# P times V as two 64-column tiles and softmax denominators as four 32-column tiles in a hybrid decoder trunk

## The chip, the cores and the metric

The kernel runs on all 8 cores of one Trainium2 chip (two dies, cores 0 to 3 and 4 to 7). Each core works through one of the 8 batch rows; no core waits for another. The metric is device microseconds of the slowest core, and the kernel before takes about 8,530 us.

A run can fall into a slow state: the cores of one die, or of both, show a lower granted TensorE clock and take longer. In group 1 of the experiments the kernel before took 8,528.1 us in its fast run, with all cores at a mean clock of 0.978 or 0.979, and 9,839.3 us in its slowest, with one die at 0.805 or 0.806 and the other at 0.977 to 0.979. Most runs of my experiments fell into it. I therefore give two numbers for each: its fast run, where there is one, and the median of its undisturbed cores. By undisturbed I mean the cores of a die on which all four had a mean granted clock of 0.970 or more, whatever the other die did. The kernel before shows that these can be compared: undisturbed cores took 8,453 to 8,533 us beside a slow die, and 8,457 to 8,530 us in fast runs.

The engines: PE is TensorE, ACT ScalarE, DVE VectorE, POOL GpSimd, SP SyncE (it issues most DMAs, 5,756 of 5,988 on core 4 of the kernel before). PEld in the profile is PE's loading of weights, which overlaps with matmuls: on the page of the kernel before, PE is busy for 94% of the span and PEld for 41%.

## The reference, cut to what matters

Four layers, each with an input projection, causal multi-head latent attention with 8 heads beside a short convolution, an output projection, a squared-ReLU MLP, and a gated per-layer embedding. The change touches only the attention:

```python
# SEQ = 4096, N_HEADS = 8, QK_HEAD = 96, V_HEAD = 64
sc = jnp.einsum('bqhd,bkhd->bhqk', qb, k, preferred_element_type=jnp.float32) * scale
sc = jnp.where(k_idx[None, :] <= q_idx[:, None], sc, -jnp.inf)
pr = jax.nn.softmax(sc, axis=-1).astype(v.dtype)
return jnp.einsum('bhqk,bkhd->bqhd', pr, v)
```

## The kernel before

Everything is held transposed: tokens lie along the free dimension, 512 queries to a block. For a pair of heads and a chunk of 128 keys the kernel makes scores S (keys x queries) on TensorE, takes the exponential on ScalarE into a tile `pt` (128 x 512, bf16), and multiplies V by it, accumulating over the chunks in PSUM. The denominator comes with the same matmul: V of a head pair is stored as 192 columns, `values of head 0 | 64 ones | values of head 1`, and a head uses 128 neighbouring columns. So one matmul with 128 columns of weights fills 64 rows of PSUM with values and 64 rows with the sum of the exponentials.

```python
# th_S: scores of one head and one key chunk
mm(ps, ps.ap[:, 0:n], kt.ap[0:96, hh, (kc % 4) * 128:(kc % 4) * 128 + 128],
   qt.ap[0:96, hh, qoff:TB], qr + [kt, qt], True, True, n=n)
# ... expt(): pt = exp(SCALE * ps) on ACT, triangle mask on POOL for the diagonal chunks

# th_PV: 128 columns of V and ones
mm(O[hh], O[hh].ap[:, qoff:TB], vt.ap[:, kc % 4, 64 * hh:64 * hh + 128], pt.ap[:, 0:n],
   [pt, vt], kc == 0, kc == nkc - 1, n=n)

# tail: after the last chunk of a head pair
act(rd, rd.ap[64:128], O[0].ap[64:128, :], AF.Ln, [O[0]])
act(rd, rd.ap[0:64], O[1].ap[0:64, :], AF.Ln, [O[1]])
act(re, re.ap[0:64], rd.ap[64:128], AF.Exp, [rd], scale=-1.0)
act(re, re.ap[64:128], rd.ap[0:64], AF.Exp, [rd], scale=-1.0)
tt("dve", lo, lo.ap, O[0].ap[0:64, :], re.ap[0:64], ALU.mult, [O[0], re, au])
tt("dve", hi, hi.ap, O[1].ap[64:128, :], re.ap[64:128], ALU.mult, [O[1], re, au])
# ...
```

Attention does not run alone. The program is put in order ahead of time by a list scheduler in the kernel's own Python code: projections of later blocks (A), attention (B) and output projection plus MLP of earlier blocks (C) are threads, and the scheduler gives TensorE whichever of their matmuls can start first by its table of costs. The order is then fixed for each engine. Two PSUM banks hold scores, two the accumulators of a head pair, four the rest.

Of the kernel before, what the change touches and what calls it, by code (L numbers as in the profile page):

```python
# [7 lines left out]
BF16 = mybir.dt.bfloat16  # L8
# [7 lines left out]
TB = 512  # L16
# [13 lines left out]
    return int(_GOFF[kind] + l * _GW[kind] + i)  # L30

C_ONES, C_BLK2, C_BLK16, C_KST, C_TRI = 0, 128, 256, 384, 448
NCB = 576
C_INVF, C_SGN = 576, 577
NCM = 578

def mk(method, *args, **kw):
    return lambda e: getattr(e, method)(*args, **kw)  # L38
# [357 lines left out]
def build(nl=NL, S=SEQ):  # L396
# [19 lines left out]
    QN = dram("QN", [4, 128, S])  # L416
    QR = dram("QR", [2, 128, S])
    KD = dram("KD", [2, 4, 96, NB, 2, TB])
    VD = dram("VD", [2, 4, 128, NK * 192])
    MIX = dram("MIX", [8, 128, S])  # L420
    CSD = dram("CSD", [2, NB, 8, 16, TB], F32)

    with contextlib.ExitStack() as st:
# [31 lines left out]
        okp = A.pool("ok", 3, BF16, [TB])  # L455
        ropq = A.pool("rope", 2, BF16, [TB])
        cosp = A.pool("cosp", 1, F32, [2, TB])
        vtp = A.pool("vt", 2, BF16, [4, 3, 64])
        kp = A.pool("k", 3, BF16, [2, TB], parts=96)
        vp = A.pool("v", 3, BF16, [4, 192])  # L460
        qp = A.pool("q", 2, BF16, [2, TB], parts=96)
        ptp = A.pool("pt", 6, BF16, [TB])
        aup = A.pool("au", 4, F32, [TB])
        anp = A.pool("an", 2, BF16, [TB])
        mxp = A.pool("mix", 8, BF16, [TB])
# [9 lines left out]
        tokC = Pool("tokC", [T() for _ in range(3)])  # L475
        build.sbuf = A.off

        qsub, ausub = {}, {}
        for t in qp.tiles:
            qsub[t] = (T(t.ap[0:64]), T(t.ap[64:80]), T(t.ap[80:96]))  # L480
        for t in aup.tiles:
            ausub[t] = (T(t.ap[0:64]), T(t.ap[64:128]))

        dks = {}

        def dk(*key):
# [12 lines left out]
            c = gcol(kind, l, i)  # L499
            return gp.ap[lo:hi, c:c + 1]  # L500

        def mm(ps, out, lhsT, rhs, reads, start, stop, n=TB):
            X.cur.grp.done += n / 512.0
            return P.c("pe", mk("matmul", out, lhsT=lhsT, rhs=rhs, start=start, stop=stop),
                       reads=reads, writes=[ps], n=n)
# [101 lines left out]
        P.dma("sp", mk("dma_start", out=gp.ap, in_=gpack), writes=[gp], nbytes=1 << 17)  # L607
        cms = [xp.tiles[i] for i in range(8, 10)]
        P.dma("sp", mk("dma_start", out=cms[0].ap, in_=cmat[:, 0:512]), writes=[cms[0]], nbytes=1 << 18)
        P.dma("sp", mk("dma_start", out=cms[1].ap[:, 0:64], in_=cmat[:, 512:576]), writes=[cms[1]], nbytes=1 << 15)  # L610
        P.dma("sp", mk("dma_start", out=cf.ap, in_=cmat[:, 576:578]), writes=[cf], nbytes=1 << 12)
        cb2 = T(cb.ap)
        P.c("dve", mk("tensor_copy", out=cb.ap[:, 0:512], in_=cms[0].ap), reads=[cms[0]], writes=[cb])
        P.c("dve", mk("tensor_copy", out=cb.ap[:, 512:576], in_=cms[1].ap[:, 0:64]), reads=[cms[1]], writes=[cb])
        P.c("dve", mk("memset", epsc.ap, EPS), writes=[epsc], n=1)
        for vt in vtp.tiles:
            P.c("pool", mk("memset", vt.ap, 1.0), writes=[vt], n=768)
        INVF = cf.ap[:, 0:1]
        SGN = cf.ap[0:32, 1:2]

# [100 lines left out]
        def th_A(s, grp):  # L721
# [190 lines left out]
            def vproj():  # L912
                for i in range(4):
                    ps = yield from bank(tokA, kvn, [("ukv", s)])
                    pc = bk[("ukv", s)]
                    for kc in range(2):
                        mm(ps, ps.ap[:, :], kvn[kc].ap[:, i * 128:(i + 1) * 128],
                           pc.ap[:, kc * 1024 + 512:kc * 1024 + 1024], [pc, kvn[kc]], kc == 0, kc == 1)
                    piece_use("ukv")
                    (vt,) = yield R("act", reads=[ps], acq=[vtp])  # L920
                    act(vt, vt.ap[:, :, 0:3:2, :], ps.ap[:, :].rearrange("p (a b x) -> p a b x", b=2, x=64), AF.Copy, [ps])
                    drop(ps)
                    kc_ = 4 * t + i
                    yield R("sp", reads=[vt], writes=[dk("VD", par, t)])
                    dma(VD[par][:, :, kc_ * 192:(kc_ + 1) * 192].rearrange("a p n -> p a n"),
                        vt.ap.rearrange("p a b x -> p a (b x)"), [vt], [dk("VD", par, t, i)], 1 << 18)
                    release(vtp, vt)
                    bump("V")

# [148 lines left out]
        def th_Bload():  # L1078
            for s in range(NS):
                l, t = divmod(s, NB)  # L1080
                par = l % 2
                for p in range(4):
                    (qt,) = yield R("sp", acq=[qp], evs=[("Q", s)])
                    a, b, c = qsub[qt]
                    dma(a.ap, QN[p].rearrange("(hh i) s -> i hh s", hh=2)[:, :, cols(t)], [dk("QN", t, p)], [a, qt], 1 << 17)
                    for j, tl in ((0, b), (1, c)):
                        dma(tl.ap, QR[j].rearrange("(h i) s -> i h s", i=16)[:, 2 * p:2 * p + 2, cols(t)],
                            [dk("QR", t, j)], [tl], 1 << 15)
                    bk[("q", s, p)] = qt
                    fire(("q", s, p))  # L1090
                    for cj in range(t + 1):
                        evs = [("K", s), ("V", s)] if cj == t else []
                        (kt,) = yield R("sp", acq=[kp], evs=evs)
                        kk_ = [dk("KD", par, cj, p, i) for i in range(3)]
                        dma(kt.ap, KD[par, p, :, cj], kk_, [kt], 96 * 2 * TB * 2)
                        bk[("k", s, p, cj)] = kt
                        fire(("k", s, p, cj))
                        (vt,) = yield R("sp", acq=[vp], evs=evs)
                        dma(vt.ap.rearrange("p a n -> p (a n)"), VD[par][p][:, cj * 768:(cj + 1) * 768],
                            [dk("VD", par, cj, i) for i in range(4)], [vt], 128 * 768 * 2)  # L1100
                        bk[("v", s, p, cj)] = vt
                        fire(("v", s, p, cj))

# [36 lines left out]
        def th_PV(s, grp):  # L1140
# [3 lines left out]
            aus = [None] * 4  # L1144
            q = SqSum(4)

            def tail(p, O):
                (rd,) = yield R("act", reads=O, acq=[rp])
                act(rd, rd.ap[64:128], O[0].ap[64:128, :], AF.Ln, [O[0]])
                act(rd, rd.ap[0:64], O[1].ap[0:64, :], AF.Ln, [O[1]])  # L1150
                (re,) = yield R("act", reads=[rd], acq=[rp])
                act(re, re.ap[0:64], rd.ap[64:128], AF.Exp, [rd], scale=-1.0)
                act(re, re.ap[64:128], rd.ap[0:64], AF.Exp, [rd], scale=-1.0)
                release(rp, rd)
                (au,) = yield R("dve", reads=[re] + O, acq=[aup])
                lo, hi = ausub[au]
                tt("dve", lo, lo.ap, O[0].ap[0:64, :], re.ap[0:64], ALU.mult, [O[0], re, au])
                tt("dve", hi, hi.ap, O[1].ap[64:128, :], re.ap[64:128], ALU.mult, [O[1], re, au])
                release(psO, O[0])
                release(psO, O[1])  # L1160
                release(rp, re)
                aus[p] = au
                yield from sq_add(q, au.ap, [au, lo, hi])

            def norm():
                rt = yield from rstd(q, 1.0 / 512, tokA)
                for c in range(4):
                    au = aus[c]
                    lo, hi = ausub[au]
                    (an,) = yield R("dve", reads=[lo, hi, rt], acq=[anp])  # L1170
                    stt(an, an.ap, au.ap, G(G_OA, l, c), rt.ap, ALU.mult, ALU.mult, [au, lo, hi, rt, gp])
                    lo.r.append(an.w)
                    hi.r.append(an.w)
                    release(aup, au)
                    yield R("sp", reads=[an], writes=[dk("MIX", t, c)])
                    dma(MIX[c][:, cols(t)], an.ap, [an], [dk("MIX", t, c)], 1 << 17)
                    release(anp, an)
                release(rp, rt)
                fire(("attn", s))

            spawn(norm(), grp, "bnorm")
            for p in range(4):
                O = [None, None]
                for kc in range(nkc):
                    cj = kc // 4
                    r = kc - 4 * t
                    qoff = 128 * r if r > 0 else 0
                    n = TB - qoff
                    for hh in range(2):
                        if kc == 0:  # L1190
                            (O[hh],) = yield R("pe", acq=[psO], evs=[("pt", s, i), ("v", s, p, cj)])
                        yield R("pe", evs=[("pt", s, i), ("v", s, p, cj)])
                        pt = bk.pop(("pt", s, i))
                        vt = bk[("v", s, p, cj)]
                        yield R("pe", reads=[pt, vt])
                        mm(O[hh], O[hh].ap[:, qoff:TB], vt.ap[:, kc % 4, 64 * hh:64 * hh + 128], pt.ap[:, 0:n],
                           [pt, vt], kc == 0, kc == nkc - 1, n=n)
                        release(ptp, pt)
                        i += 1
                    if kc % 4 == 3:  # L1200
                        release(vp, bk.pop(("v", s, p, cj)))
                spawn(tail(p, O), grp, "tail")
            fire(("B", s))

        def th_Bseq():
# [368 lines left out]
```

## Time and profile before

| | before |
|---|---|
| median of runs | 8,533.7 us (8,506.4 to 8,577.0, 4 runs) |
| TensorE busy | 7,994.5 us, 94% |
| ScalarE, VectorE busy | 62%, 47% |
| TensorE idle | 525.9 us |
| start to start of neighbouring 128x512 matmuls, median | 216 ns |

The page of the kernel before, its first part (busy time of each engine), the engines' line of its fourth (the chain that ended last), and TensorE's two groups of its fifth (busy us, mean ns of one, idle time before them and what ended most of it):

```profile
PE 7994.5 (94%) x36480; PEld 3514.0 (41%) x36480; DVE 3975.2 (47%) x5969; ACT 5325.5 (62%) x10023; POOL 1075.5 (13%) x1582
...
PE 77%; ACT 8%; DMA 5%; issue 4%; SPq 2%; DVE 2%; POOL 1%; ACTq 0%; DVEq 0%; POOLq 0%
...
L38 PE MATMUL ps<-arena 128*128 128x512 bf16 (+2 forms) x36480 | 7994.5, 378 | 525.9 <-ACT arena L38 220.5
L38 PEld LDWEIGHTS ps<-arena 128*128 128x128 bf16 (+2 forms) x36480 | 3514.0, 98 | 5005.9 <-issue 1147.3
```

TensorE is what the kernel waits for. The mean of 378 ns is how long the profile shows one matmul and not what it costs: the next one starts 216 ns after it, so that matmuls overlap, and the cost is these 216 ns. The stretches of 2,000 us show that this holds through the run. Columns are the stretch, its length, busy time and count of PE, PEld, DVE, ACT and POOL, then granted clock, DMA share and GB/s:

```profile
0.00:2000.00 2000.00, 1684.32 (x7388) 715.77 (x7389) 904.27 (x1385) 1254.20 (x2375) 247.98 (x411) 0.93 0.79 195
2000.00:4000.00 2000.00, 1932.44 (x8890) 853.23 (x8888) 961.67 (x1440) 1316.22 (x2492) 272.11 (x394) 0.99 0.71 196
4000.00:6000.00 2000.00, 1931.23 (x8915) 856.06 (x8914) 978.06 (x1463) 1305.71 (x2461) 271.63 (x394) 0.99 0.72 198
```

The kernel before has one place where the shape of the weights changes: the rotary key's, with eight matmuls of 64 columns and, elsewhere and alone, one of 32 rows and 64 columns. The timeline of PEld around one of these (start us, length, what, count, and the idle time before it):

```profile
3662.92 0.10 PEld L38 LDWEIGHTS ps<-arena 128*128 128x128 bf16 x1
3663.44 1.43 PEld L38 LDWEIGHTS ps<-arena 128*64 128x64 bf16 x8 [0.43 <-issue]
3665.29 0.77 PEld L38 LDWEIGHTS ps<-arena 128*128 128x128 bf16 x5 [0.41 <-issue]
```

The weight loader stands idle for over 0.4 us at the way in and at the way out. In this trace it does not load ahead across the change of shape. In the starts of the matmuls this is 309 ns from the last 128-column one to the first 64-column one, and 312 ns back, in place of 216. The lone 32-row matmul costs 309 ns in and 331 ns out.

Last, what TensorE waited for (the view of waits, core 4: total us, times, longest us):

```profile
PE ps L38 <- ACT arena L38: 220.5, 245, 15.5
PE ps L38 <- DVE arena L38: 139.4, 109, 22.4
PE ps L38 <- DMA arena<-WZ_B: 64.7, 9, 26.7
```

### The profile page before, as it was taken

What the parts mean: (1) busy time and instruction counts of PE and PEld (TensorE: products, weight loads), DVE (VectorE), ACT (ScalarE), POOL (GpSimd) and SP (SyncE); (2) the same over time, 40 slices, a digit from 0 to 9 for tenths busy, and PEclk for the clock granted to TensorE, in tenths of its full rate; (3) what the DMA queues carried; (4) which work ended last, traced back from release to release, by engine and by line L of the source; (5) the groups of instructions that cost most, each with busy time, mean ns of one, the idle gap of its engine ahead of it and who ended that gap; (6) DMA issues with size and microseconds to landing.
All of it is one profiled execution on the core that took longest, in us unless ns stands there. A gap on an engine that the chain in (4) does not pass through costs nothing.

```text
span 8529.4 us, 132287 instructions; the slowest of 8 cores (8475.2 to 8529.4 us)
## 1 busy us (share of the span) xinstructions
PE 7994.5 (94%) x36480; PEld 3514.0 (41%) x36480; DVE 3975.2 (47%) x5969; ACT 5325.5 (62%) x10023; POOL 1075.5 (13%) x1582
## 2 busy tenths in 40 slices
PE   4589999999999999999999999999999999999998
PEld 1233344444444444444444444444444444444443
DVE  3445544445554444444555544444555544443334
ACT  3457766677555677666566666767655666766523
POOL 0111111012111111101111110111111011101001
PEclk7799999999999999999999999999999999999999
DMA  9998886666888866656788875566666666655554
GB/s 179 184 206 220 222 209 179 177 185 190 216 209 212 208 195 189 184 163 180 208 224 218 214 205 171 179 187 187 183 196 179 191 184 186 182 164 169 160 171 140
DMA packets 833341, 1621.95 MB, mean 190 GB/s; under 512 B 161472, under 2 KB 436544, under 8 KB 830016
## 3 DMA queue, kind: packets, MB, share of 16 engines
q1 hardware_dynamic: 813504, 1496.31, 60.2%
q0 software_dynamic: 19136, 117.19, 9.3%
q8 instruction: 331, 5.42, 0.3%
q14 instruction: 370, 3.03, 0.1%
HBM read 1524.77 MB, written 314.31 MB: 216 GB/s over the span
## 4 chain that ended last, share of the span: by engine, by line
PE 77%; ACT 8%; DMA 5%; issue 4%; SPq 2%; DVE 2%; POOL 1%; ACTq 0%; DVEq 0%; POOLq 0%
PE ps L38 77%; ACT arena L38 8%; SPq L38 2%; DVE arena L38 2%; DMA arena<-xT 2%; DMA MIX<-arena 1%; DMA arena<-WZ_B 1%; POOL arena L38 1%; DMA QN<-arena 0%; DMA HD<-arena 0%; DMA arena<-WC_B 0%; DMA QR<-arena 0%; ACTq L200 0%; DMA VD<-arena 0%; DMA arena<-VD 0%
## 5 line engine op out<-in xcount | busy, mean ns | idle before, releaser
L38 PE MATMUL ps<-arena 128*128 128x512 bf16 (+2 forms) x36480 | 7994.5, 378 | 525.9 <-ACT arena L38 220.5
L38 PEld LDWEIGHTS ps<-arena 128*128 128x128 bf16 (+2 forms) x36480 | 3514.0, 98 | 5005.9 <-issue 1147.3
L38 ACT ACTIVATE arena<-ps 128x512 bf16<-128x512 f32 (+5 forms) x6976 | 3605.3, 573 | 2632.6 <-PE ps L38 2502.0
L38 DVE TENSOR_TENSOR arena<-arena 128x512 bf16<-128x512 f32 (+3 forms) x2176 | 1564.6, 728 | 1735.4 <-ACT arena L38 1688.1
L38 ACT ACTIVATE arena<-arena 128x512 f32<-128x512 f32 (+2 forms) x2498 | 1540.4, 629 | 462.0 <-DVE arena L38 284.5
L38 POOL TENSOR_TENSOR arena<-arena 128x128 bf16<-128x128 bf16 (+2 forms) x1344 | 944.7, 715 | 5607.6 <-ACT arena L38 3752.6
L38 DVE TENSOR_TENSOR arena<-arena,ps 128x512 f32<-128x512 f32 x1280 | 872.1, 685 | 1521.3 <-PE ps L38 1384.4
L38 DVE SCALAR_TENSOR_TENSOR arena<-arena 128x512 bf16<-128x512 f32 (+2 forms) x1540 | 1120.3, 765 | 536.4 <-ACT arena L38 324.8
L38 DVE SCALAR_TENSOR_TENSOR arena<-ps,arena 128x512 bf16<-128x512 f32 (+1 forms) x320 | 239.3, 748 | 486.8 <-ACT arena L38 444.7
L38 ACT ACTIVATE arena<-ps,arena 128x512 f32<-128x512 f32 (+1 forms) x544 | 375.2, 690 | 84.0 <-PE ps L38 82.7
L38 DVE TENSOR_TENSOR arena<-ps,arena 64x512 f32<-64x512 f32 x256 | 176.2, 688 | 249.1 <-ACT arena L38 245.0
L38 POOL DMA_DIRECT2D WC_B<-wc x164 | 85.2, 520 | 1555.8 <-PE ps L38 1467.2
L38 DVE TENSOR_SCALAR arena<-arena 128x512 f32<-128x512 f32 x135 | 65.4, 485 | 0.9 <-issue 0.2
L38 DVE COPY arena<-arena 128x2 f32<-128x2 f32 x240 | 46.5, 194 | 12.2 <-DVE arena L38 1.4
L38 POOL DMA_DIRECT2D WZ_B<-wz x24 | 13.3, 555 | 160.6 <-PE ps L38 160.6
L38 POOL DMA_DIRECT2D arena<-pT x32 | 24.6, 769 | 24.2 <-PE ps L38 18.1
L38 POOL DMA_DIRECT2D WU_B<-wu x12 | 6.7, 555 | 100.8 <-PE ps L38 82.0
L38 ACT ACT_TABLE_LOAD x5 | 6.4, 1283 | 19.0 <-DMA arena<-xT 13.8
L38 DVE CAST arena<-arena 128x512 f32<-128x512 int32 (+2 forms) x5 | 1.9, 379 | 6.8 <-DMA arena<-cmat 6.4
L38 POOL MEMSET arena<- 128x768 bf16 x2 | 1.4, 737 | 0.3 <-POOLq L400 0.3
L38 DVE MEMSET arena<- 128x2 f32 (+1 forms) x17 | 1.0, 60 | 0.0
L400 POOL MEMSET const-float32-0.0<- 128x1 f32 x1 | 0.1, 99 | 0.5 <-issue 0.5
(3 smaller groups left out, 0.3 us busy)
## 6 DMA issues: line engine op xcount, KB each, us to landing
arena<-WC_B SPq DMA_DIRECT2D x1312, 512.0 KB, 4.4
arena<-WZ_B SPq DMA_DIRECT2D x544, 256.0 KB, 4.5
arena<-KD SPq DMA_DIRECT2D x576, 192.0 KB, 4.2
arena<-VD SPq DMA_DIRECT2D x576, 192.0 KB, 4.3
WC_B<-wc POOLq DMA_DIRECT2D x164, 512.0 KB, 8.6
outT<-arena SPq DMA_DIRECT2D x256, 256.0 KB, 4.0
arena<-outT SPq DMA_DIRECT2D x192, 256.0 KB, 5.5
arena<-xT SPq DMA_DIRECT2D x160, 256.0 KB, 7.7
```

The costliest lines, as they stand in the source:

```text
L38: return lambda e: getattr(e, method)(*args, **kw)
L400: nc = bass.Bass("TRN2", target_bir_lowering=False, dynamic_dma_scratch_size=2048)
```

## The change

The intent is to stop spending 64 columns of the array on copies of one sum. The values of the two heads become two matmuls with 64 columns each, placed in different halves of the array's columns so that they might run at once. The denominators of two heads and two key chunks become four matmuls with 32 columns of ones, also side by side. If they do run at once, a head pair needs 3 slots of TensorE for two chunks in place of 4. The price: V loses its ones (128 columns, a third less to load), the denominators of even and odd chunks lie in different groups of 32 rows and must be swapped and added in the tail, and a head pair asks for both accumulator banks before its first matmul, where the kernel before asked for the second one a matmul later (both kernels hold a bank until the tail has read it).

```diff
-        vp = A.pool("v", 3, BF16, [4, 192])
+        vp = A.pool("v", 3, BF16, [4, 128])
-        ptp = A.pool("pt", 6, BF16, [TB])
+        ptp = A.pool("pt", 8, BF16, [TB])
@@ mm: the scheduler's cost of a tile is its share of a slot
-        def mm(ps, out, lhsT, rhs, reads, start, stop, n=TB):
+        def mm(ps, out, lhsT, rhs, reads, start, stop, n=TB, par=1):
+            n = n // par
@@ tail
-                (rd,) = yield R("act", reads=O, acq=[rp])
-                act(rd, rd.ap[64:128], O[0].ap[64:128, :], AF.Ln, [O[0]])
-                act(rd, rd.ap[0:64], O[1].ap[0:64, :], AF.Ln, [O[1]])
-                ...
+                (rd,) = yield R("act", reads=[Dn], acq=[rp])
+                for j in range(4):
+                    k = j ^ 1
+                    act(rd, rd.ap[32 * j:32 * j + 32], Dn.ap[32 * k:32 * k + 32, :], AF.Copy, [Dn])
+                yield R("dve", reads=[rd, Dn])
+                tt("dve", rd, rd.ap, rd.ap, Dn.ap[:, :], ALU.add, [rd, Dn])
+                release(psO, Dn)
+                yield R("act", reads=[rd])
+                act(rd, rd.ap, rd.ap, AF.Ln, [rd])
+                act(rd, rd.ap, rd.ap, AF.Exp, [rd], scale=-1.0)
+                (au,) = yield R("dve", reads=[rd, O], acq=[aup])
+                tt("dve", au, au.ap, O.ap[:, :], rd.ap, ALU.mult, [O, rd])
+                release(psO, O)
@@ th_PV
+                    if kc == 0:
+                        O, Dn = yield R("pe", acq=[psO, psO], evs=evs)
+                    yield R("pe", evs=evs)
+                    pt = [bk.pop(("pt", s, i + hh)) for hh in range(2)]
+                    ...
                     for hh in range(2):
-                        mm(O[hh], O[hh].ap[:, qoff:TB], vt.ap[:, kc % 4, 64 * hh:64 * hh + 128], pt.ap[:, 0:n], ...)
+                        mm(O, O.ap[64 * hh:64 * hh + 64, qoff:TB], vt.ap[:, kc % 4, 64 * hh:64 * hh + 64], pt[hh].ap[:, 0:n],
+                           [pt[hh], vt], kc == 0, kc == nkc - 1, n=n, par=2)
+                    pts += [(pt[hh], qoff, n) for hh in range(2)]
+                    ... # t == 0: two matmuls with zero weights open the odd quadrants
+                    if kc % 2 == 1:
+                        for j, (ptj, qo, nj) in enumerate(pts):
+                            row = 64 * (j % 2) + 32 * (j // 2)
+                            mm(Dn, Dn.ap[row:row + 32, qo:TB], ONE32, ptj.ap[:, 0:nj], [ptj, cb], kc == 1 and (t > 0 or j < 2),
+                               kc == nkc - 1, n=nj, par=4)
+                            release(ptp, ptj)
+                        pts = []
```

More of the change, by code (lines that the diff above doesn't have):

```diff
@@ L32 @@
 C_ONES, C_BLK2, C_BLK16, C_KST, C_TRI = 0, 128, 256, 384, 448
-NCB = 576
-C_INVF, C_SGN = 576, 577
-NCM = 578
+C_ZERO = 576
+NCB = 608
+C_INVF, C_SGN = 608, 609
+NCM = 610
 def mk(method, *args, **kw):
@@ L418, in build @@
     KD = dram("KD", [2, 4, 96, NB, 2, TB])
-    VD = dram("VD", [2, 4, 128, NK * 192])
+    VD = dram("VD", [2, 4, 128, NK * 128])
     MIX = dram("MIX", [8, 128, S])
@@ L457, in build @@
         cosp = A.pool("cosp", 1, F32, [2, TB])
-        vtp = A.pool("vt", 2, BF16, [4, 3, 64])
+        vtp = A.pool("vt", 2, BF16, [TB])
         kp = A.pool("k", 3, BF16, [2, TB], parts=96)
-        vp = A.pool("v", 3, BF16, [4, 192])
+        vp = A.pool("v", 3, BF16, [4, 128])
         qp = A.pool("q", 2, BF16, [2, TB], parts=96)
-        ptp = A.pool("pt", 6, BF16, [TB])
+        ptp = A.pool("pt", 8, BF16, [TB])
         aup = A.pool("au", 4, F32, [TB])
@@ L476, in build @@
         build.sbuf = A.off
-        qsub, ausub = {}, {}
+        qsub = {}
         for t in qp.tiles:
             qsub[t] = (T(t.ap[0:64]), T(t.ap[64:80]), T(t.ap[80:96]))
-        for t in aup.tiles:
-            ausub[t] = (T(t.ap[0:64]), T(t.ap[64:128]))
         dks = {}
@@ L609, in build @@
         P.dma("sp", mk("dma_start", out=cms[0].ap, in_=cmat[:, 0:512]), writes=[cms[0]], nbytes=1 << 18)
-        P.dma("sp", mk("dma_start", out=cms[1].ap[:, 0:64], in_=cmat[:, 512:576]), writes=[cms[1]], nbytes=1 << 15)
-        P.dma("sp", mk("dma_start", out=cf.ap, in_=cmat[:, 576:578]), writes=[cf], nbytes=1 << 12)
+        P.dma("sp", mk("dma_start", out=cms[1].ap[:, 0:96], in_=cmat[:, 512:608]), writes=[cms[1]], nbytes=1 << 15)
+        P.dma("sp", mk("dma_start", out=cf.ap, in_=cmat[:, 608:610]), writes=[cf], nbytes=1 << 12)
         cb2 = T(cb.ap)
         P.c("dve", mk("tensor_copy", out=cb.ap[:, 0:512], in_=cms[0].ap), reads=[cms[0]], writes=[cb])
-        P.c("dve", mk("tensor_copy", out=cb.ap[:, 512:576], in_=cms[1].ap[:, 0:64]), reads=[cms[1]], writes=[cb])
+        P.c("dve", mk("tensor_copy", out=cb.ap[:, 512:608], in_=cms[1].ap[:, 0:96]), reads=[cms[1]], writes=[cb])
         P.c("dve", mk("memset", epsc.ap, EPS), writes=[epsc], n=1)
-        for vt in vtp.tiles:
-            P.c("pool", mk("memset", vt.ap, 1.0), writes=[vt], n=768)
         INVF = cf.ap[:, 0:1]
@@ L920, in vproj @@
                     (vt,) = yield R("act", reads=[ps], acq=[vtp])
-                    act(vt, vt.ap[:, :, 0:3:2, :], ps.ap[:, :].rearrange("p (a b x) -> p a b x", b=2, x=64), AF.Copy, [ps])
+                    act(vt, vt.ap, ps.ap[:, :], AF.Copy, [ps])
                     drop(ps)
@@ L924, in vproj @@
                     yield R("sp", reads=[vt], writes=[dk("VD", par, t)])
-                    dma(VD[par][:, :, kc_ * 192:(kc_ + 1) * 192].rearrange("a p n -> p a n"),
-                        vt.ap.rearrange("p a b x -> p a (b x)"), [vt], [dk("VD", par, t, i)], 1 << 18)
+                    dma(VD[par][:, :, kc_ * 128:(kc_ + 1) * 128].rearrange("a p n -> p a n"),
+                        vt.ap.rearrange("p (a n) -> p a n", n=128), [vt], [dk("VD", par, t, i)], 1 << 17)
                     release(vtp, vt)
@@ L1098, in th_Bload @@
                         (vt,) = yield R("sp", acq=[vp], evs=evs)
-                        dma(vt.ap.rearrange("p a n -> p (a n)"), VD[par][p][:, cj * 768:(cj + 1) * 768],
-                            [dk("VD", par, cj, i) for i in range(4)], [vt], 128 * 768 * 2)
+                        dma(vt.ap.rearrange("p a n -> p (a n)"), VD[par][p][:, cj * 512:(cj + 1) * 512],
+                            [dk("VD", par, cj, i) for i in range(4)], [vt], 1 << 17)
                         bk[("v", s, p, cj)] = vt
@@ L1145, in th_PV, with tail @@
             q = SqSum(4)
-            def tail(p, O):
-                (rd,) = yield R("act", reads=O, acq=[rp])
-                act(rd, rd.ap[64:128], O[0].ap[64:128, :], AF.Ln, [O[0]])
-                act(rd, rd.ap[0:64], O[1].ap[0:64, :], AF.Ln, [O[1]])
-                (re,) = yield R("act", reads=[rd], acq=[rp])
-                act(re, re.ap[0:64], rd.ap[64:128], AF.Exp, [rd], scale=-1.0)
-                act(re, re.ap[64:128], rd.ap[0:64], AF.Exp, [rd], scale=-1.0)
-                release(rp, rd)
-                (au,) = yield R("dve", reads=[re] + O, acq=[aup])
-                lo, hi = ausub[au]
-                tt("dve", lo, lo.ap, O[0].ap[0:64, :], re.ap[0:64], ALU.mult, [O[0], re, au])
-                tt("dve", hi, hi.ap, O[1].ap[64:128, :], re.ap[64:128], ALU.mult, [O[1], re, au])
-                release(psO, O[0])
-                release(psO, O[1])
-                release(rp, re)
+            def tail(p, O, Dn):
+                (rd,) = yield R("act", reads=[Dn], acq=[rp])
[11 more added lines that the diff above has]
+                release(psO, O)
+                release(rp, rd)
                 aus[p] = au
-                yield from sq_add(q, au.ap, [au, lo, hi])
+                yield from sq_add(q, au.ap, [au])
             def norm():
@@ L1168, in norm @@
                     au = aus[c]
-                    lo, hi = ausub[au]
-                    (an,) = yield R("dve", reads=[lo, hi, rt], acq=[anp])
-                    stt(an, an.ap, au.ap, G(G_OA, l, c), rt.ap, ALU.mult, ALU.mult, [au, lo, hi, rt, gp])
-                    lo.r.append(an.w)
-                    hi.r.append(an.w)
+                    (an,) = yield R("dve", reads=[au, rt], acq=[anp])
+                    stt(an, an.ap, au.ap, G(G_OA, l, c), rt.ap, ALU.mult, ALU.mult, [au, rt, gp])
                     release(aup, au)
@@ L1181, in th_PV @@
             spawn(norm(), grp, "bnorm")
+            ONE32 = cb.ap[:, C_ONES:C_ONES + 32]
             for p in range(4):
-                O = [None, None]
+                O = Dn = None
+                pts = []
                 for kc in range(nkc):
@@ L1188, in th_PV @@
                     n = TB - qoff
-                    for hh in range(2):
-                        if kc == 0:
-                            (O[hh],) = yield R("pe", acq=[psO], evs=[("pt", s, i), ("v", s, p, cj)])
-                        yield R("pe", evs=[("pt", s, i), ("v", s, p, cj)])
-                        pt = bk.pop(("pt", s, i))
-                        vt = bk[("v", s, p, cj)]
-                        yield R("pe", reads=[pt, vt])
-                        mm(O[hh], O[hh].ap[:, qoff:TB], vt.ap[:, kc % 4, 64 * hh:64 * hh + 128], pt.ap[:, 0:n],
-                           [pt, vt], kc == 0, kc == nkc - 1, n=n)
-                        release(ptp, pt)
-                        i += 1
+                    evs = [("pt", s, i), ("pt", s, i + 1), ("v", s, p, cj)]
+                    if kc == 0:
+                        O, Dn = yield R("pe", acq=[psO, psO], evs=evs)
+                    yield R("pe", evs=evs)
+                    pt = [bk.pop(("pt", s, i + hh)) for hh in range(2)]
+                    i += 2
+                    vt = bk[("v", s, p, cj)]
+                    yield R("pe", reads=pt + [vt])
+                    for hh in range(2):
+                        mm(O, O.ap[64 * hh:64 * hh + 64, qoff:TB], vt.ap[:, kc % 4, 64 * hh:64 * hh + 64], pt[hh].ap[:, 0:n],
+                           [pt[hh], vt], kc == 0, kc == nkc - 1, n=n, par=2)
+                    pts += [(pt[hh], qoff, n) for hh in range(2)]
+                    if t == 0 and kc == 0:
+                        for j in range(2):
+                            mm(Dn, Dn.ap[64 * j + 32:64 * j + 64, :], cb.ap[:, C_ZERO:C_ZERO + 32], pt[j].ap,
+                               [pt[j], cb], True, False, par=2)
+                    if kc % 2 == 1:
[4 more added lines that the diff above has]
+                            release(ptp, ptj)
+                        pts = []
                     if kc % 4 == 3:
                         release(vp, bk.pop(("v", s, p, cj)))
-                spawn(tail(p, O), grp, "tail")
+                spawn(tail(p, O, Dn), grp, "tail")
             fire(("B", s))
```

## The prediction

> **What bounds it now.** TensorE. The page gives PE 7994.5 us busy of 8529.4 (94%); ACT has 62%, DVE 47%. The chain that ended last is 77% PE. From 1600 us on the 400 us windows show PE 375 to 395 us busy at a granted clock of 0.97 to 1.00. Successive 128x512 matmuls start 216 ns apart (median of start-to-start times in the trace), so weight loads hide. PE idle is 526 us, some 205 of it in the first 400 us. What PE costs in start-to-start time is what the kernel costs.
>
> **What the change removes.** Before, a head's P.V is one 128-column matmul, half values and half ones: 4 slots of 216 ns for two key chunks of a head pair. After, if tiles really run side by side, 2 slots for the values and 1 for four denominators. Counting columns in the two instruction streams: 35,680 slots fall to 34,632, so 1,048 x 0.216 = 226 us off PE. [...]
>
> **What it adds on PE.** The array changes its tile shape. [...] This trace shows it already, in the eight 64-column matmuls of the rotary key: 128 to 64 columns starts 309 ns after the last 128-wide matmul, back again 312 ns after, against 216 within either shape. So each change costs 93 to 96 ns. The program before has 128 changes. In the new PE order they number 5,739, because the scheduler puts other work between the pairs: 2,206 bursts of two 64-column matmuls, 1,152 of four 32-column ones. 5,611 x 94 ns = 527 us (estimate). [...] the second tile of a pair should start about 27 ns late and the fourth of a quad about 80 late: 2,200 x 27 + 1,150 x 80 = 150 us (estimate).
>
> **Rest.** ACT gets two more operations in each of 128 tails (about 0.6 us each, 150 us in all), hidden at 62%. The value loads shrink by a third; the DMA part of the chain is 5%, so 0 to 20 us. The next head pair waits for both PSUM banks of a longer tail (four copies, add, Ln, Exp, multiply): 20 to 40 us if other matmuls don't fill it. A slower PE hides part of today's waits of PE[...]: minus 100 us.
>
> **Sum.** 8517 - 226 + 527 + 150 + 30 - 100 - 15 = about 8880 us, slower by 4%; nearly all of the PE terms lie on the critical path. Range 8680 to 9090. Chances: faster by over 2% 0.05, within 2% 0.10, slower 0.85.
>
> **What would show it.** Start-to-start medians: 128 to 64 near 309 ns, 64 to 32 near 300, back to 128 near 312; within a pair 25 to 60 ns (216 would mean no overlap). PE's share stays at 94% or above although fewer columns stream; ACT's falls to about 61%. Granted clock unchanged.
>
> **What would make it wrong.** [...] Tiles of different moving data may not overlap: then 9,800 us or more. Second tiles could start late, by an exposed weight load of 100 ns each: 9,100 to 9,200. Waits for the exponentials, which now need both heads before a pair starts, could matter.

The sum came to 8,517 - 226 + 527 + 150 + 30 - 100 - 15, or about 8,880 us. These terms stand on less than the others: that tiles run side by side (in the 226 us) was an assumption; the 27 and 80 ns (in the 150 us) are estimates, near the 28 to 29 ns between loads that the trace has, but for loads of one tile; and 30 and -100 us are my estimates, for which the record gives no numbers to work them out from (that a change of shape costs nothing where it falls into a wait was not shown). A cut sentence allowed for a change of shape that costs less in a short burst than in one of eight matmuls, with a time near the old one or 1 to 2% faster. The 100 ns of an exposed weight load is PEld's mean of 98 ns.

## The result

The changed kernel took 8,901.5 us in the median of 4 runs (8,888.9 to 8,931.0), against 8,533.7 us: 368 us or 4.3% slower (ratio 1.0431, 95% interval 1.0376 to 1.0486). Ratios are the mean time of one kernel's fast runs over that of the other's of the same rounds, so they are not quite the ratio of the medians. The prediction was 8,880 us.

The same parts of the page, after:

```profile
PE 8388.6 (94%) x41120; PEld 3319.2 (37%) x41120; DVE 3930.5 (44%) x5969; ACT 5507.2 (62%) x10279; POOL 1072.5 (12%) x1580
...
PE 82%; ACT 7%; DMA 4%; issue 3%; SPq 2%; DVE 1%; POOL 0%; ACTq 0%; DVEq 0%; POOLq 0%
...
L39 PE MATMUL ps<-arena 128*128 128x512 bf16 (+5 forms) x41120 | 8388.6, 382 | 489.9 <-ACT arena L39 236.6
...
L39 PEld LDWEIGHTS ps<-arena 128*128 128x128 bf16 (+3 forms) x41120 | 3319.2, 99 | 5558.8 <-issue 2486.4
```

TensorE streams fewer columns and yet is busy 394 us longer, with its share still 94%. The weight loader loads less, but its idle time that nothing in the profile explains ("issue") has grown from 1,147 to 2,486 us. That is the place to look. The timeline of PEld in a stretch of attention, core 2:

```profile
3445.68 0.11 PEld L39 LDWEIGHTS ps<-arena 128*64 128x64 bf16 x2 [0.42 <-issue]
3446.02 0.11 PEld L39 LDWEIGHTS ps<-arena 96*128 96x128 bf16 x2 [0.23 <-issue]
3446.56 0.11 PEld L39 LDWEIGHTS ps<-arena 128*64 128x64 bf16 x2 [0.43 <-issue]
3446.89 0.10 PEld L39 LDWEIGHTS ps<-arena 128*32 128x32 bf16 x4 [0.23 <-issue]
3447.22 0.33 PEld L39 LDWEIGHTS ps<-arena 128*128 128x128 bf16 x3 [0.23 <-issue]
```

Each line is a change of shape with an idle stretch before it. From the pair's loads at 3446.56 to those of the four ones tiles at 3446.89, and from there to the next full weights at 3447.22, it is 0.33 us each, where a slot takes 0.216 us.

The starts of the matmuls give the cost of each kind of change. I took these from the trace's start times: the medians from a matmul with 512 columns of moving data to the next matmul (core 4; "128" includes the scores' 96-row matmuls, "64" leaves out the lone 32-row one):

| from, to | before: count, ns | after: count, ns | over 216 ns |
|---|---|---|---|
| 128 to 128 | 34,598, 216 | 28,839, 216 | 0 |
| 128 to 64 | 30, 309 | 1,951, 309 | 93 |
| 64 to 64, second tile of a pair | none | 1,883, 3 | side by side |
| 32 to 32, next tile of four | none | 2,960, 3 | side by side |
| 64 to 32 | none | 912, 333 | 117 |
| 64 to 128 | 32, 312 | 983, 336 | 120 |
| 32 to 128 | none | 870, 322 | 106 |

The tiles do run side by side: a second tile starts 3 ns after the first. A pair between full matmuls costs 309 + 3 + 336 = 648 ns from the full matmul before it to the one after. That is exactly 3 x 216: the full matmul before it and two more slots. The pair saves a slot and pays a slot. 842 times a pair stands like this in the trace, with a median of 648 ns. Where the four ones tiles follow the pair (821 times), the way from full matmul to full matmul takes 978 ns, 330 more. So pairs that stand alone break even, and what is lost is about the price of the denominators, which came free before: 1,152 x 330 ns = 380 us (an estimate from these medians).

From the same start times I made a ledger of TensorE's time from its first matmul to its last, on core 4 of both runs. "Slots" is the columns streamed, at 2.4 per ns and counted once for tiles side by side, plus 2.5 ns for each matmul. Both figures are estimates, fitted to the medians of the kernel before, 216, 165, 112 and 59 ns for 512, 384, 256 and 128 columns: 128 columns more take 51 to 53 ns more, which is 2.4 to 2.5 per ns, and with 2.5 ns for each matmul 512 columns come to 216. For the four lengths they give 216, 162.5, 109 and 56 ns. "Shape changes" is what a start that follows another shape is late, up to 150 ns; "waits" is lateness over 150 ns within one shape, and what exceeds 150 ns at a change. "Rest" is what remains.

| us, core 4 | slots | shape changes (number) | waits | rest | sum |
|---|---|---|---|---|---|
| before | 7,709.5 | 13.1 (128) | 723.0 | 51.9 | 8,497.5 |
| after | 7,504.6 | 626.0 (5,739) | 665.4 | 42.9 | 8,838.9 |
| difference | -204.9 | +612.9 | -57.6 | -9.0 | +341.4 |

Slots and shape changes are the same on every core whose records are complete (1 to 5 and 7), waits are not: 670 to 723 us before and 658 to 682 after. Core 4 has the longest before, so its -57.6 is too favourable; by the medians of these cores it is -21.

What the view of waits puts down to other engines, core 4, after:

```profile
PE ps L39 <- ACT arena L39: 243.4, 243, 15.6
PE ps L39 <- DVE arena L39: 134.9, 87, 21.7
PE ps L39 <- DMA arena<-WZ_B: 54.2, 5, 25.5
```

I expected a slower TensorE to wait for others less (in split64, below, it did, by 166 us). Its waits for ScalarE have not fallen, they have grown from 220.5 to 243.4 us (177 to 221 before and 228 to 243 after on the six complete cores). This is the second thing that the experiments were made for.

Granted clock plays no part: 0.99 in both kernels in the two stretches from 2,000 to 6,000 us. After:

```profile
2000.00:4000.00 2000.00, 1937.41 (x9606) 766.10 (x9605) 900.15 (x1366) 1297.42 (x2436) 262.23 (x389) 0.99 0.65 182
4000.00:6000.00 2000.00, 1933.84 (x9569) 771.84 (x9568) 927.80 (x1410) 1278.55 (x2394) 256.63 (x372) 0.99 0.66 185
```

### The profile page after: what moved, and what is told of

The parts are those of the page before. It is cut to its first block, busy times and chain, and to the rows that moved or that the text cites. A ratio compares the mean times of both kernels' runs of the same rounds, so it can differ in the third digit from the quotient of the medians.

```text
span 8887.3 us, 142023 instructions; the slowest of 8 cores (8846.5 to 8887.3 us)
## 1 busy us (share of the span) xinstructions
PE 8388.6 (94%) x41120; PEld 3319.2 (37%) x41120; DVE 3930.5 (44%) x5969; ACT 5507.2 (62%) x10279; POOL 1072.5 (12%) x1580
## 4 chain that ended last, share of the span: by engine, by line
PE 82%; ACT 7%; DMA 4%; issue 3%; SPq 2%; DVE 1%; POOL 0%; ACTq 0%; DVEq 0%; POOLq 0%
PE ps L39 82%; ACT arena L39 7%; SPq L39 2%; DVE arena L39 1%; DMA arena<-xT 1%; DMA MIX<-arena 1%; DMA arena<-WZ_B 1%; POOL arena L39 0%; DMA QN<-arena 0%; DMA VD<-arena 0%; DMA QR<-arena 0%; DMA HD<-arena 0%; ACTq L201 0%; DMA arena<-KD 0%; DVEq L201 0%
## 5 line engine op out<-in xcount | busy, mean ns | idle before, releaser
L39 PE MATMUL ps<-arena 128*128 128x512 bf16 (+5 forms) x41120 | 8388.6, 382 | 489.9 <-ACT arena L39 236.6
L39 ACT ACTIVATE arena<-ps 128x512 bf16<-128x512 f32 (+5 forms) x7232 | 3814.9, 572 | 2910.3 <-PE ps L39 2770.6
L39 PEld LDWEIGHTS ps<-arena 128*128 128x128 bf16 (+3 forms) x41120 | 3319.2, 99 | 5558.8 <-issue 2486.4
L39 DVE TENSOR_TENSOR arena<-arena 128x512 bf16<-128x512 f32 (+3 forms) x2176 | 1532.9, 713 | 2007.7 <-ACT arena L39 1960.8
L39 DVE TENSOR_TENSOR arena<-arena,ps 128x512 f32<-128x512 f32 x1408 | 960.8, 686 | 1859.3 <-PE ps L39 1492.6
L39 DVE SCALAR_TENSOR_TENSOR arena<-arena 128x512 bf16<-128x512 f32 (+1 forms) x1540 | 1120.3, 764 | 494.7 <-ACT arena L39 317.9
L39 DVE TENSOR_TENSOR arena<-ps,arena 128x512 f32<-128x512 f32 x128 | 88.4, 691 | 95.0 <-ACT arena L39 94.8
```

Source lines behind the costliest of these rows:

```text
L39: return lambda e: getattr(e, method)(*args, **kw)
```

## The experiments

The theory: the changes of tile shape cost about 610 us, and this outweighs the saved slots. Rivals: the longer tail with its ScalarE work and its hold on two banks; waiting for the exponentials of both heads before a pair; or simply another order out of the scheduler. All twelve runs (ten new kernels, the changed one and best8 a second time) computed the correct result. They ran in three groups, each on one chip, with the kernel before on the same chip each time:

| kernel | fast run, us | undisturbed cores: median us (dies) | over before's undisturbed cores |
|---|---|---|---|
| before, group 1 | 8,528.1 | 8,512 (7) | |
| split64 | 9,246.0 | 9,236 (6) | +724 |
| beforeburst2 | 8,590.1 | 8,552 (5) | +40 |
| burst2 | 8,737.2 | 8,715 (6) | +203 |
| burst4 | 8,647.4 | 8,626 (4) | +114 |
| before, group 2 | 8,501.8; 8,513.2; 8,531.8 | 8,488 (9) | |
| afterfold | none | 8,764 (3) | +276 |
| burst4v32 | none | 8,530 (3) | +42 |
| best4 | 8,485.2 | 8,469 (5) | -19 |
| best8 | 8,407.2 | 8,394 (5) | -94 |
| before, group 3 | none | 8,511 (3) | |
| after_again | none | 8,882 (7) | +371 |
| beforetail | 8,658.2 | 8,633 (6) | +122 |
| before_cost | 8,559.4 | 8,513 (3) | +2 |
| best8_again | 8,438.7 | 8,416 (6) | -95 |

A few further runs (burst4v32 with both dies at a clock of 0.87 to 0.88, burst4 with one at 0.96, best4 with one at 0.96, after_again, 8,942 us, with one at 0.968 to 0.971) I leave out of the column of fast runs. Only best4 got a ratio with an interval, and that includes such a run: 1.003, 0.987 to 1.019.

In the fast runs of the kernel before and of the changed one, all eight cores ran at a mean clock of 0.97 to 0.98, and the profiled cores at 0.99 from 2,000 to 6,000 us. By the traces' own clock records, 0.81 held for 594 to 729 us on the cores of burst4's slowed die, for 91 and 98 us on two cores of the kernel before, and never in the profile of the changed kernel. The two stretches of burst4's core 1, whose clock is the last but two of the numbers, are the same kernel on the same core in one run, first with the lower clock and then without it:

```profile
8000.00:8180.00 180.00, 180.00 (x813) 70.80 (x811) 46.24 (x69) 83.56 (x159) 7.26 (x16) 0.82 0.39 115
6000.00:6180.00 180.00, 177.05 (x949) 74.18 (x947) 78.94 (x124) 120.87 (x233) 13.16 (x22) 1.00 0.60 171
```

### split64: the tiles without the rest of the change

```diff
 # kernel before, th_PV
-                        mm(O[hh], O[hh].ap[:, qoff:TB], vt.ap[:, kc % 4, 64 * hh:64 * hh + 128], pt.ap[:, 0:n], ...)
+                        P.c("pe", mk2(*[((O[hh].ap[64 * j:64 * j + 64, qoff:TB],),
+                                         dict(lhsT=vt.ap[:, kc % 4, 64 * (hh + j):64 * (hh + j) + 64], rhs=pt.ap[:, 0:n],
+                                              start=kc == 0, stop=kc == nkc - 1)) for j in range(2)]),
+                            reads=[pt, vt], writes=[O[hh]], n=n)
```

`mk2` issues two matmuls as one operation of the program, so that the order and the waits stay those of before.

> The kernel before, in its own order of operations and with its own 192-column V layout, tail and banks; only each P.V matmul is issued as two 64-column tiles side by side (values and ones). Same arithmetic, same slots. In its PE order the P.V matmuls stand in 4,261 separate bursts, 4,057 of them single. Theory (changes of the tile shape cost): each burst pays 93 ns going in, 3 ns for the second tile and about 120 ns coming out, so 4,261 x 0.216 = 920 us more, less up to 100 us that falls into waits: 9350 to 9460 us, slower by 10 to 11%. Rivals (the longer tail, the wait for two banks or for both heads, the extra ScalarE work, the new order): nothing of theirs is in this kernel, so it stays within 0.5% of 8534 us.

Measured: 9,246 us in its fast run, +724 us by undisturbed cores, 8.5% slower. The same arithmetic, in the same order, with the short tail, with nothing but the shape changed, costs more than the whole change did. PEld's timeline (core 2, an undisturbed die) shows full weights and pairs in turn, 0.33 us apart in place of 0.216:

```profile
5001.15 0.10 PEld L38 LDWEIGHTS ps<-arena 96*128 96x128 bf16 x1 [1.44 <-issue]
5001.48 0.11 PEld L41 LDWEIGHTS ps<-arena 128*64 128x64 bf16 x2 [0.24 <-issue]
5001.82 0.10 PEld L38 LDWEIGHTS ps<-arena 96*128 96x128 bf16 x1 [0.23 <-issue]
```

The ledger of core 2 has 8,594 changes for 940 us, as expected (927 us over before). But waits were 515 us, where the kernel before has 681 us on the same core (723 on core 4): 166 us less. I had allowed 100 us for waits that a slower TensorE hides, and it hid more; hence the time below the range that I had expected. So the theory holds for the cost of the changes, and one more thing is learnt: with the tail kept short, the slower TensorE did wait much less, 515 us in place of 681.

### beforeburst2, burst2, burst4: fewer changes of shape

```diff
 # changed kernel, th_PV (burst4; burst2 has 2 in place of 4 and keeps 8 buffers)
-                for kc in range(nkc):
+                for k0 in range(0, nkc, 4):
+                    # wait for the 8 exponentials, then without a break:
+                    # the value pairs of 4 chunks, then the ones tiles of 4 chunks
-        ptp = A.pool("pt", 8, BF16, [TB])
+        ptp = A.pool("pt", 10, BF16, [TB])
```

beforeburst2 groups the full 128-column matmuls of two chunks in the kernel before in the same manner, with 7 buffers.

> The kernel before with full 128-column P.V matmuls, but those of two key chunks (four matmuls) issued together once all four exponentials are there, with 7 instead of 6 exponential buffers. No change of tile shape is added. Theory: grouping alone is worth nothing, 8534 us within 0.7%. Rival (grouping itself helps, through the order or fewer waits): faster by 1 to 3%; rival (waiting for several exponentials is what costs): slower by over 1%.

> The changed kernel with the same matmuls, tiles, tail and buffers; only the value pairs of two key chunks are issued together, just before their denominators. Changes of tile shape fall from 5,739 to 3,561. Theory: 1,061 fewer entries x 93 ns, 1,087 fewer exits from 64 columns x 120 ns = 229 us less: about 8670 us, ratio to before 1.016. Rivals (tail, banks, ScalarE): they are untouched, so about 8900 us.

> As the last, with four key chunks together and 10 exponential buffers. Changes of tile shape 1,840. Theory: 1,632 x 93 + 592 x 117 + 547 x 106 + 1,084 x 120 ns = 409 us less than the changed kernel: about 8490 us, ratio to before 0.995. If waits for eight exponentials at once cost something, 8530 to 8600. Rivals (tail, banks, ScalarE): about 8900 us.

Measured: beforeburst2 8,590 us, +40 us, so grouping alone gains nothing and costs a little. burst2 8,737 us, +203 us. Against after_again's +371 us, on another chip, it gained 168 us, where 229 were expected. burst4 8,647 us, +114 us, a gain of 257 us where 409 were expected. The rivals, for which burst2 and burst4 should have stayed at 8,900 us, are out as the main cause. The ledgers say where the missing gain went:

| us | slots | shape changes (number) | waits | rest |
|---|---|---|---|---|
| after, core 4 | 7,504.6 | 626.0 (5,739) | 665.4 | 42.9 |
| burst2, core 4 | 7,500.9 | 364.1 (3,561) | 702.9 | 60.8 |
| burst4, core 5 | 7,510.9 | 178.8 (1,840) | 822.9 | 44.3 |

The shape changes fell by 262 and 447 us, even more than I had worked out. A long burst also makes its way out cheaper: in burst4 it takes 312 ns from the last 32-column tile to a full matmul, not 322, and 309 ns from 64 to 32, not 333. But waits grew by 38 and 158 us. Core 4 is mild here: by the median of cores 4, 5 and 7, three complete cores, waits grew by 90 us in burst2 and 208 in burst4, and with these the account nearly closes (-172 and -239 us, against gains of 168 and 257 measured). In the waits of burst4's core 5, TensorE's for ScalarE are 287.6 us against 243.4 in the changed kernel. Whoever takes eight exponentials at once gives eight buffers back at once, and the scores that fill them again come in a bunch; that reading of the waits is argued, not shown.

### afterfold and beforetail: the tail

```diff
 # afterfold: changed kernel, tail
-                for j in range(4):
-                    k = j ^ 1
-                    act(rd, rd.ap[32 * j:32 * j + 32], Dn.ap[32 * k:32 * k + 32, :], AF.Copy, [Dn])
                 yield R("dve", reads=[rd, Dn])
+                for j in range(4):
+                    k = j ^ 1
+                    P.c("dve", mk("tensor_copy", out=rd.ap[32 * j:32 * j + 32], in_=Dn.ap[32 * k:32 * k + 32, :]), ...)
```

> The changed kernel; only the four partition-swapping copies of each tail go from ScalarE to VectorE (512 copies of 0.59 us, 301 us of ScalarE). Changes of tile shape stay at about 5,700. Theory as predicted (shape changes carry the loss, the longer tail was put at 20 to 40 us): 8860 to 8900 us. Rival (the tail and its ScalarE work carry a good part of the 370 us): 8830 us or less; if they carried it all, about 8530 us.

Measured: no fast run, undisturbed cores 8,764 us, +276 us. The changed kernel has +371 us by the same measure, so having the four copies on ScalarE and not on VectorE cost it about 95 us. By the ledger of core 4, nothing else moved: 5,702 changes of shape for 620.6 us, slots 7,506.0, but waits 542.8 us in place of 665.4. Waits of TensorE, afterfold, core 4:

```profile
PE ps L39 <- ACT arena L39: 148.1, 219, 14.7
PE ps L39 <- DVE arena L39: 122.3, 100, 20.9
```

Those for ScalarE have fallen from 243.4 to 148.1 us, and the copies, 301 us of ScalarE before, are 352 us of VectorE now and cost less there. My 20 to 40 us for the tail was too little. But this is not the price of the longer tail against that of the kernel before: afterfold's tail has two ScalarE operations fewer than the kernel before, the changed kernel's two more. The opposite test adds to the kernel before what the change added to ScalarE's tail:

```diff
 # beforetail: kernel before, tail; both results are overwritten by the Ln that follow
                 (rd,) = yield R("act", reads=O, acq=[rp])
+                act(rd, rd.ap[0:64], O[0].ap[64:128, :], AF.Copy, [O[0]])
+                act(rd, rd.ap[64:128], O[1].ap[0:64, :], AF.Copy, [O[1]])
```

> The kernel before with two dead ScalarE copies of 64 rows (one of each accumulator) at the head of each tail, overwritten at once, so that a tail has six ScalarE operations as in the changed kernel. No tiles change. Theory after afterfold (the tail's ScalarE work, 125 us in the changed kernel, is paid by TensorE in waits): 8570 to 8650 us, about 80 us over before. As I predicted it at first (20 to 40 us at most, otherwise hidden at 62% busy): 8530 to 8560 us.

Measured: 8,658 us, +122 us. The 256 dead copies are 151 us of ScalarE in the trace (591 ns each), and four fifths of that shows up in the kernel's time although ScalarE is busy only 62%. The ledger of core 4 has waits of 857.8 us in place of 723.0 and nothing else changed. Waits of TensorE, beforetail, core 4:

```profile
PE ps L38 <- ACT arena L38: 272.3, 300, 13.1
PE ps L38 <- DVE arena L38: 152.4, 115, 22.2
PE ps L38 <- DMA arena<-WZ_B: 83.0, 9, 25.3
```

Both tests say that work on ScalarE at the end of a head pair is not hidden: four fifths of it was paid for in beforetail, and in afterfold a third (95 of 301 us) was got back by moving it to another engine. They don't say by which way: the work delays the exponentials, it holds the accumulator banks longer, and it changes the order that the scheduler finds. That stays open.

### burst4v32, best4, best8, before_cost: a version that beats both

burst4v32 issues V too as 32-column tiles, four side by side (two halves for two heads), so that values and denominators have one shape and a burst has one way in and one way out.

```diff
 # burst4v32 against burst4
-                            mm(O, O.ap[64 * hh:64 * hh + 64, qo:TB], vt.ap[:, kc % 4, 64 * hh:64 * hh + 64], ..., par=2)
+                            for d in range(2):
+                                o = 64 * hh + 32 * d
+                                mm(O, O.ap[o:o + 32, qo:TB], vt.ap[:, kc % 4, o:o + 32], ..., par=4)
```

> As burst4 (8647 us in its undisturbed run), but the values too go as 32-column tiles, four side by side (two halves of V for two heads), so that a group needs one shape: 1,275 changes of shape instead of 1,840. Theory: 565 x 94 ns = 53 us less, 4,608 more matmuls x 3 ns = 14 us more: 8610 us. If side-by-side work of four different weight tiles is slower than of two, more than 8650 us.

Measured: +42 us by undisturbed cores, so 72 us less than burst4; 39 were expected. Four matmuls side by side in place of two did no harm here.

```diff
 # best4: burst4v32 with afterfold's tail, and
-                        O, Dn = yield R("pe", acq=[psO, psO], evs=evs)
+                        (O,) = yield R("pe", acq=[psO], evs=evs)
+                        # ... (Dn,) = yield R("pe", acq=[psO]) just before the first ones tiles
-            return 0.06 + n / 1200.0, 0.19 + n / 1200.0      # scheduler's cost of ACT
+            return 0.095 + n / 1200.0, 0.19 + n / 1200.0
-            return 0.075 + n * f / 960.0, 0.155 + n * f / 960.0   # and of DVE
+            return 0.13 + n * f / 960.0, 0.16 + n * f / 960.0
 # best8: burst4v32 with afterfold's tail, cost of ACT 0.095, 0.3, of DVE as above, and
-                for k0 in range(0, nkc, 4):
+                for k0 in range(0, nkc, 8):
+                    g = min(8, nkc - k0)
+        pt: 18 buffers; ringA 4 in place of 5, ringC 4 in place of 5, r 4 in place of 5
```

> burst4v32 with the tail's copies on VectorE, the second accumulator bank asked for only where the denominators start, and the scheduler's cost figures for ScalarE and VectorE nearer the measured ones. Changes of shape about 1,450. Theory: what bursts lost against their sum of shape changes (burst4: 8647 against 8490 us) are waits of TensorE for ScalarE, which this eases by 60 to 100 us: 8500 to 8550 us, as the kernel before. If waits aren't eased: 8610 us.

> The same with up to eight key chunks in a burst, 18 exponential buffers, one slot less in three other pools; 768 changes of shape. Theory: about 500 fewer changes than burst4v32 x 95 ns = 48 us, and the cheaper tail 40 to 80 us: 8470 to 8540 us, ratio to before 0.994 to 1.001. If the smaller weight rings starve TensorE: 8600 us or more.

Measured: best4 8,485 us, -19 us, no difference that I would defend. best8 8,407 us, -94 us, which is below the range that I had expected. Repeated on another chip:

> best8 once more for an interval: its undisturbed cores took 8350 to 8430 us and its one fast run 8407 us, so ratio to before 0.985 to 0.990.

8,439 us in its one fast run and -95 us by undisturbed cores, so 1.1% faster than before on both chips (8,394 over 8,488 and 8,416 over 8,511, 0.989). The cores do not overlap: in group 2 best8's undisturbed cores took 8,351 to 8,427 us and those of before 8,453 to 8,530 us. The page of best8, first part, and the engines' line of its chain:

```profile
PE 7852.1 (93%) x45728; PEld 3396.7 (40%) x45728; DVE 4286.2 (51%) x6481; ACT 5156.5 (61%) x9767; POOL 1076.4 (13%) x1580
...
PE 80%; ACT 6%; DMA 5%; DVE 3%; issue 3%; SPq 3%; POOL 0%; ACTq 0%; DVEq 0%; POOLq 0%
```

Its ledger (core 3): slots 7,520.7, shape changes 75.0 us (768), waits 774.8, rest 4.5. Against before it saves 189 us of slots and 47 of rest, pays 62 for shapes and 52 in waits (the rest falls because "slots" charges 2.5 ns to every tile, while in a burst four tiles start 3 ns apart and the next four 206 ns later, 215 in all).

Part of best8 is the scheduler's better cost figures, which have nothing to do with tiles. The control:

> The kernel before with nothing but the scheduler's cost figures of best8. If best8's lead over before came from these figures, this too is near 8410 us; if it comes from the tiles in long bursts, this is within 0.7% of before, 8470 to 8590 us.

Measured: 8,559 us, undisturbed cores +2 us. The figures alone are worth nothing to the kernel before. That best8's gain comes from the long bursts in one shape, with their buffers, together with the cheap tail is what is left; I didn't run each part of it singly.

### after_again

> The changed kernel once more, on the same chip as the next three, so that its undisturbed dies can be set beside theirs: cores of 8846 to 8890 us, as in its first profile; 8890 to 8930 us in a fast run.

Undisturbed cores took 8,843 to 8,903 us, median 8,882, against 8,869 us for the median core of the first four runs. The difference to before, +371 us, repeats.

## Why the prediction was right

The time was right, 8,880 against 8,901.5 us, and so was the mechanism: changes of shape cost more than the saved slots. That it came within 22 us is luck: the terms below miss by 20 to 70 us each and in both directions. Step by step:

- **The bound.** Right. Before and after, TensorE is at 94%, and a cost on it alone (split64) of 927 us in the ledger comes through at 724.
- **Saved slots, 226 us.** Nearly: 205 us by the ledger. That tiles overlap was an assumption, and held: the next tile starts 3 ns later.
- **The cost of a change.** "So each change costs 93 to 96 ns" was read off eight-matmul bursts of another part of the kernel. In the short bursts of the change it was 93 ns going in, 117 between 64 and 32 columns, 106 and 120 coming out. By so much the first start after each change is late; what happens in the array meanwhile the trace doesn't show.
- **The second tile's delay.** "The second tile of a pair should start about 27 ns late and the fourth of a quad about 80 late" failed: a further tile starts 3 ns late. (The clause that derived the 27 ns read 26 ns between loads of successive tiles off the trace, which has 28 to 29 ns between two 64-column loads of one tile and no tiles side by side.) That the sum for a pair was right all the same, 27 + 312 against 3 + 336, is luck. The 24 ns at the way out are not shown to belong to the second tile: the lone 32-row matmul of the kernel before, which has no second tile, takes 331 ns out, and after four pairs in a row (burst4) the way from 64 to 32 columns takes 309 ns in place of 333. For quads the 80 ns was too dear: 3 x 3 ns inside and 322 out. Together, changes and delay were put at 527 + 150 = 677 us and measured 613.
- **The tail.** "20 to 40 us if other matmuls don't fill it", and its ScalarE work "hidden at 62%", was the step that failed. Its ScalarE copies cost about 95 us more than the same copies on VectorE by undisturbed cores (afterfold), 123 us in the ledger's waits of one core, and two more ScalarE operations cost 122 us in the kernel before (beforetail).
- **Waits that a slower TensorE hides.** "Minus 100 us" was too small too. With the tail as it was (split64), waits fell by 166 us on the same core. What was seen after the change, -58 us on core 4 and -21 by the median core, I read as such a fall less what the tail gave back. Two wrong terms of the sum, 30 - 100, came near the net that was measured; that, too, is luck.
- **DMA, 0 to 20 us.** Value loads are 128 KB in place of 192; no run tested whether that is worth anything.
- **Other signs.** Starts of 128 to 64 near 309 ns: right. 64 to 32 near 300: 333. Back near 312: 322 to 336. ScalarE to 61%: it stayed at 62%. Clock unchanged: right.

## What to carry to other kernels

Before splitting a matmul into tiles that run side by side, count how often TensorE's order will change shape, and price each change by the start-to-start time of one that is already in the trace, from a burst as short as yours (the long bursts of this trace gave 93 to 96 ns, and the short ones of the change cost up to 120); here a change cost 93 to 120 ns, about half of a 216 ns slot, so a pair of tiles that stands alone gained nothing, and of the bursts only those of up to eight key chunks in one shape paid (two and four chunks in two shapes still lost). If you tile, use one shape for all that stands together (burst4v32 took 72 us less than burst4), and issue the burst without a break. And don't call work hidden because its engine is 62% busy (of 151 us added to ScalarE, 122 showed up in the time): ask what the dependent engine does while it lasts, by adding a dead copy of that work to the kernel that you have.
